# RWKV chunk transitions formed in bulk: W, P, Q and R ahead of the chunk loop, and small products laid on four 64x64 quarters of the PE array

## The chip, the core and the metric

The kernel runs on one core of a Trainium2 chip. A core has a matrix engine (TensorE, here PE, with its weight loads listed apart as PEld), three engines for element-wise work (VectorE or DVE, ScalarE or ACT, GpSimd or POOL) and DMA queues, which it issues from SyncE (SP). Matrix products are written to PSUM, an accumulator memory of eight banks; DVE and ACT carry them from there to SBUF. The metric is the time of one execution on the device in microseconds (us).

## The reference

Two layers, 512 tokens of 1024 channels, float32. Each layer normalises, projects, runs four mixers on the projection and mixes their outputs. The change lies in one of the four, an RWKV-7 time mix of 8 heads of 64 channels, run in both directions:

```
def _wkv7_scan(r, w, k, v, a, bb):
    def step(S, inp):
        r_t, w_t, k_t, v_t, a_t, b_t = inp
        sa = jnp.einsum("bhvk,bhk->bhv", S, a_t)
        S = S * w_t[:, :, None, :] + sa[..., None] * b_t[:, :, None, :] + v_t[..., None] * k_t[:, :, None, :]
        return S, jnp.einsum("bhvk,bhk->bhv", S, r_t)
    _, y = lax.scan(step, S0, (tm(r), tm(w), tm(k), tm(v), tm(a), tm(bb)))
```

The state S is a 64x64 matrix for each head. The other mixers are a Mamba-2 scan, differential attention and grouped-query attention.

## The kernel before

A layer runs in three parts: the RWKV mixer (`rwkv`), with the attention mixers woven into it; the Mamba mixer (`ssd`); the output projection (`accumulate`, `finish`). `rwkv` walks over four **blocks** j, each two heads (index e, 64 channels on each half of the 128 partitions), both directions d and all 512 tokens as 8 **chunks** of 64. So a block has 2 x 2 x 8 = 32 chunk problems.

In chunk form the scan of a block becomes these products, all 64x64x64 in float32 (the trace shows each such product as two matmul records and two weight loads):

- `products`: A and B matrices within a chunk (tile `pa`, 128 columns each), masked by DVE into `AT[0]` (from b) and `AT[1]` (from k).
- `turned`: v and the b, k matrices with tokens on the partitions (tiles `p5`, in the trace `p<-cst,lv`, and `pt`), carried by ACT into V2 and BKT.
- The inverse T of a unit triangular matrix: its 16x16 diagonal blocks are solved on DVE (15 pairs of small operations, lines 541 and 543), between transposes of 32x32 blocks on DVE (lines 528, 549, 551). Then come one product M (tile `ch<-DN,AT`) and three products that refine T (`ch<-DT,Mp`, `ch<-TT,Mp`), each followed by a DVE addition (line 571).
- Bulk terms: x (`px`), KV (`pk`), Y0 (`py`).
- The **chain** over the 8 chunks cc. With S the state of one chunk it forms X = a S + x (tile `bk`, DVE line 624), U = T X (`bk`, DVE copy line 635), S' = lambda (b U + S) + KV (`bk`, DVE lines 633 and 640), and adds r S and (b r) U to the output bank (`yb`). These are three steps that wait for each other, each a small group of products and a DVE operation.

Two things fill the time between these steps. `ahead()` advances the element-wise preparation of the next block (`prep`) and the normalisation of the last one (`norm`) by one piece. `fill(us)` advances attention work (tiles `pjt`, `pjc`, `sc`, `ptp`, `ob`) by a credit of about that many us; `fill.scale` is set so that 98% of 299.5 us of such work is spent in the four blocks. The constants F_SV (15 solve steps), F_MG (5 bulk steps) and F_CH (24 chain steps) say how the credit is shared out. The program text is then put in order by a scheduler that lets an instruction pass another that is not ready by its own reckoning; on the chip each engine works its list strictly in that order.

PSUM banks: two for projections (`pj`), two that all small work shares (`g`), one for attention (`ga`), two for the chain (`ch0`, `ch1`), one for the output (`yb`).

In `products` the matmul goes from half e of the partitions to half e or to the other half, e ^ m, so that four consecutive products use four different 64x64 quarters of the array. In the other products one block uses two quarters, on a diagonal.

Of the kernel before, what the change touches and what calls it, by code (L numbers as in the profile page):

```python
# [19 lines left out]
L = 512  # L20
# [7 lines left out]
F_SV = 1.5  # L28
F_MG = 2.4
F_CH = 1.7  # L30
# [7 lines left out]
C_LAG = 4  # L38
N_PR = 3
# [3 lines left out]
END = 0.98  # L43
# [13 lines left out]
C_N = C_TH + 2  # L57
# [18 lines left out]
def trunk(ctx: ExitStack, tc: tile.TileContext, x_in, win, wwd, wdt, wout, w2a, cols, rows, sscal, consts, out, dbg=None,  # L76
# [32 lines left out]
    nomask = cst[:, C_NOM:C_NOM + 64]  # L109
    th = [cst[:, C_TH + n:C_TH + n + 1] for n in range(2)]  # L110
# [141 lines left out]
    def rwkv(i, lay, pw, ps, rp, fill):  # L252
# [36 lines left out]
        AR = rp.tile([128, 4, 2, 8, 64], F32, tag="AR", name="AR")  # L289
# [26 lines left out]
        def prep(j):  # L316
# [6 lines left out]
            s["a"], s["r"] = Aa, Ar = AR[:, j % 2], AR[:, 2 + j % 2]  # L323
# [11 lines left out]
            for d in range(2):  # L335
# [41 lines left out]
                BKf = rp.tile([128, 17 * 64], F32, tag="BK", name="BK", bufs=2)  # L377
                G.memset(BKf[:, 0:64], 0.0)
                s["BK"].append(BKf)
                BK = BKf[:, 64:].rearrange("p (c a t) -> p c a t", c=8, a=2)  # L380
# [4 lines left out]
                G.tensor_tensor(BK[:, :, 1, :], v3(kp), il, op=ALU.mult)  # L385
# [4 lines left out]
                V.scalar_tensor_tensor(BK[:, :, 0, :], v3(b1), -0.5, il, op0=ALU.mult, op1=ALU.mult)  # L390
# [23 lines left out]
        AT = [rp.tile([128, 2, 8, 2, 64], F32, tag=f"AT{n}", name=f"AT{n}") for n in range(2)]  # L414
        BKT = rp.tile([128, 2, 2, 8, 64], F32, tag="BKT", name="BKT")
        V2 = rp.tile([128, 2, 8, 64], F32, tag="V2", name="V2")

        ba = AT[0][:, :, :, 0, :]
        half = [slice(0, 64), slice(64, 128)]

        def products(j, c0, n):

            ar = AR[:, j % 2:j % 2 + 3:2]
            for d in range(2):
                BK = sts[j]["BK"][d][:, 64:].rearrange("p (c a t) -> p c a t", c=8, a=2)
                pa = [ps.tile([128, n, 128], F32, tag="g", name="pa") for _ in range(2)]
                for cc in range(n):
                    for m in range(2):
                        for e in range(2):
                            mm(pa[m][half[e ^ m], cc, :].rearrange("p (a t) -> p a t", a=2), BK[half[e], c0 + cc, m, :],  # L430
                               ar[half[e], :, d, c0 + cc, :], True, True)
                for m in range(2):
                    V.tensor_tensor(AT[m][:, d, c0:c0 + n].rearrange("p c a t -> p c (a t)"), pa[m],
                                    rmask.unsqueeze(1).to_broadcast([128, n, 128]), op=ALU.mult)

        def turned(j):
            BK, v = sts[j]["BK"], sts[j]["v"]
            for d in range(2):

                p5 = ps.tile([128, 8, 64], F32, tag="g", name="p5")  # L440
                for cc in range(8):
                    for e in range(2):
                        mm(p5[half[1 - e], cc, :], v[d][half[e], cc * 64:cc * 64 + 64], ident[half[e], half[e]], True, True)
                S.activation(V2[:, d], p5, AF.Copy)
                yield
            for d in range(2):
                for e in range(2):
                    pt = ps.tile([128, 8, 64], F32, tag="g", name="pt")

                    n = 7 + e  # L450
                    for cc in range(n):
                        PE.transpose(pt[:, cc, :], BK[d][half[e], (2 * cc + 1 - e) * 64:(2 * cc + 3 - e) * 64],
                                     ident[half[e], half[e]])
                    S.activation(BKT[:, d, e, 0:n], pt[:, 0:n], AF.Copy)
                    yield
# [47 lines left out]
        fill.scale = END * 299.5 / (4 * (15 * F_SV + 5 * F_MG + 24 * F_CH) + F_GN)  # L503
        products(0, 0, 4)
        products(0, 4, 4)
        ys = None
        for j in range(4):
            Aa, Ar, lamC = (sts[j][n] for n in ("a", "r", "lamC"))
            ahead.gens = [turned(j)]
# [5 lines left out]


            sv = rp.tile([128, 1024], F32, tag="sv", name="sv", bufs=1)
# [3 lines left out]
            DT = rp.tile([128, 2, 8, 64], F32, tag="dt", name="DT", bufs=1)  # L521
            DN = rp.tile([128, 2, 8, 64], F32, tag="dn", name="DN", bufs=1)
            G.memset(sv[:, 768:1024], 0.0)
            G.memset(sv[:, 768:1024:17], 1.0)
            quad = [(slice(32 * q, 32 * q + 32), slice(32 * (q % 2), 32 * (q % 2) + 32)) for q in range(4)]
            unit = lambda t, q: t[quad[q][0], :, :, quad[q][1]].rearrange("p d c (h t) -> p t h (d c)", h=2)
# [4 lines left out]
            bam = AT[0].rearrange("p d c a t -> p (d c) a t")[:, :, 0, :]  # L531
            G.tensor_tensor(bam, bam, nomask.unsqueeze(1).to_broadcast([128, 16, 64]), op=ALU.mult)
            G.memset(DT, 0.0)
            G.memset(DN, 0.0)
            for jj in range(15):
                ahead()
                fill(F_SV)
# [8 lines left out]
            for h in range(2):  # L546
                V.tensor_scalar(Dx[:, :, h, :], Ti, th[h], None, op0=ALU.mult)
            for q in range(4):
                V.transpose(out=unit(DN, q), in_=Dx[quad[q][0]].rearrange("p t h s -> p s h t"))
            for q in range(4):  # L550
                V.transpose(out=unit(DT, q), in_=Dx[quad[q][0]])
            ahead()
            fill(F_MG)
            chd = lambda d: ps.tile([128, 8, 64], F32, tag=f"ch{d}", name=f"ch{d}")
            both = [(cc, e) for cc in range(8) for e in range(2)]

            Mp = rp.tile([128, 2, 8, 64], F32, tag="sv", name="Mp", bufs=1)
            for d in range(2):
                pm = chd(d)
                for cc, e in both:  # L560
                    mm(pm[half[e], cc, :], ba[half[e], d, cc, :], DN[half[e], d, cc, :], True, True)
                S.activation(Mp[:, d], pm, AF.Copy)
            TT = rp.tile([128, 2, 8, 64], F32, tag="dn", name="TT", bufs=1)
            for n in range(3):
                ahead()
                fill(F_MG)
                for d in range(2):
                    ph = chd(d)
                    for cc, e in both:
                        mm(ph[half[e], cc, :], Mp[half[e], d, cc, :], (TT if n else DT)[half[e], d, cc, :], True, True)  # L570
                    V.tensor_tensor(TT[:, d], ph, DT[:, d], op=ALU.add)
            ahead()
            fill(F_MG)

            KV = rp.tile([128, 2, 8, 64], F32, tag="sv", name="KV", bufs=1)
            Y0 = rp.tile([128, L], F32, tag="dt", name="Y0", bufs=1)
            for d in range(2):
                px = ps.tile([128, 8, 64], F32, tag="g", name="px")
# [853 lines left out]
```

## Time and profile before

| | |
|---|---|
| time, median of 3 runs | 1848.87 us (1847.95 to 1852.3) |
| the profiled execution: time, span of its instructions | 1854.4 us, 1852.6 us |
| PE busy | 1642.2 us, 89% of the span |
| DVE, ACT, POOL busy | 1163.1 us (63%), 810.5 us (44%), 698.9 us (38%) |
| the four blocks of layer 0 lie at | 113 to 675 us |
| those of layer 1 at | 1031 to 1593 us |

Busy is the union of an engine's instruction times. Of matmuls the trace gives start and a modelled end, so many records overlap: the time that a group of them holds the engine is read from the start of its first record to the start of the next group. "Idle before" is time in which the engine had nothing running, put down to what released the next instruction. The profile gives the clock that TensorE was granted, as a share of 2.4 GHz; its levels here are 1.0 and 0.5 (1.2 GHz).

### The profile page before, as it was taken

How to read it: one execution, taken by the hardware profiler on the slowest of the kernel's cores; microseconds unless marked ns; L12 is line 12 of the kernel's file. 1: busy time of each engine (PE TensorE's matmuls, PEld its weight loads, DVE VectorE, ACT ScalarE, POOL GpSimd, SP SyncE). 2: the span in 40 equal slices, each digit the busy share in tenths (PEclk: the TensorE clock that was granted, in tenths of full speed). 3: DMA queues.
4: the chain of work that ended last, by engine and by line, in shares of the span. 5: the costliest groups of instructions: out<-in, count | busy, mean ns of one | idle time of the engine just before them, and what ended most of it. 6: DMA issues, size and time to landing. Idle time of an engine off the chain costs nothing. (4 is left out here: it accounts for less than half of the span.)

```text
span 1852.6 us, 35939 instructions
## 1 busy us (share of the span) xinstructions
PE 1642.2 (89%) x14616; PEld 1325.0 (72%) x14616; DVE 1163.1 (63%) x2426; ACT 810.5 (44%) x1566; POOL 698.9 (38%) x728
## 2 busy tenths in 40 slices
PE   7887989998988999988897799899889898999888
PEld 6576767776767877766785677687677677778666
DVE  4587586676665437886256865956856744378852
ACT  4644245435524255442346442563444242554431
POOL 4443233334242334543354332433432323345333
PEclk9898999999989999989999989999999899999899
DMA  4111101111001114122431111011110011231223
GB/s 152 60 40 39 35 24 42 49 41 44 26 24 47 42 54 135 64 73 88 134 104 52 32 39 36 29 37 50 37 44 30 24 47 36 81 112 53 86 86 114
DMA packets 57510, 108.41 MB, mean 59 GB/s; under 512 B 6784, under 2 KB 8832, under 8 KB 57344
## 3 DMA queue, kind: packets, MB, share of 16 engines
q1 hardware_dynamic: 57344, 106.11, 17.7%
q8 instruction: 114, 1.87, 0.4%
q14 instruction: 52, 0.43, 0.1%
HBM read 95.60 MB, written 10.49 MB: 57 GB/s over the span
## 5 line engine op out<-in xcount | busy, mean ns | idle before, releaser
L144 POOL TENSOR_TENSOR wlo<-wf,whi 128x512 fp32r<-128x512 f32 x228 | 315.6, 1389 | 444.7 <-ACT whi L143 360.2
L82 PE MATMUL pjt<-whi,hhi 128*128 128x256 f32 x960 | 297.5, 310 | 13.0 <-ACT raw L269 6.5
L82 PE MATMUL pjt<-wlo,hhi 128*128 128x256 f32 x960 | 293.7, 307 | 1.1 <-POOL wlo L144 1.1
L82 PE MATMUL pjt<-whi,hlo 128*128 128x256 f32 x960 | 287.9, 300 | 0.0
L143 ACT ACTIVATE whi<-wf 128x512 fp32r<-128x512 f32 x228 | 141.3, 628 | 215.8 <-PE pjt L82 104.0
L82 PEld LDWEIGHTS pjt<-whi,hhi 128*128 128x128 f32 x960 | 192.6, 201 | 34.6 <-issue 9.0
L82 PEld LDWEIGHTS pjt<-wlo,hhi 128*128 128x128 f32 x960 | 192.6, 201 | 11.4 <-issue 6.5
L82 PEld LDWEIGHTS pjt<-whi,hlo 128*128 128x128 f32 x960 | 193.0, 201 | 8.8 <-issue 5.6
L82 PE MATMUL pjc<-hhi,whi 128*128 128x512 f32 x384 | 161.8, 421 | 9.0 <-ACT raw L269 5.2
L82 PE MATMUL pjc<-hhi,wlo 128*128 128x512 f32 x384 | 159.7, 418 | 0.0
L82 PE MATMUL pjc<-hlo,whi 128*128 128x512 f32 x384 | 158.1, 412 | 0.0
L872 DVE TENSOR_REDUCE nm<-sc 128x1 f32<-128x512 f32 x96 | 65.9, 687 | 84.6 <-PE sc L82 78.1
L875 ACT ACTIVATE p<-sc,nm 128x512 f32<-128x512 f32 x96 | 65.9, 686 | 115.1 <-DVE nm L872 114.7
L82 PE MATMUL mix<-whi,ylo 128*128 128x512 f32 x256 | 106.1, 414 | 5.4 <-DVE ylo L1216 5.4
L82 PE MATMUL sc<-qT,qT 64*128 64x512 f32 (+1 forms) x256 | 101.7, 494 | 7.2 <-ACT y L1055 3.8
L82 PE MATMUL mix<-whi,yhi 128*128 128x512 f32 x256 | 101.0, 417 | 5.1 <-ACT yhi L1215 5.1
L82 PE MATMUL mix<-wlo,yhi 128*128 128x512 f32 x256 | 104.4, 408 | 0.0
L82 PEld LDWEIGHTS pjc<-hhi,whi 128*128 128x128 f32 x384 | 76.5, 199 | 32.9 <-issue 6.6
L82 PEld LDWEIGHTS pjc<-hhi,wlo 128*128 128x128 f32 x384 | 76.3, 199 | 21.4 <-issue 4.2
L82 PEld LDWEIGHTS pjc<-hlo,whi 128*128 128x128 f32 x384 | 76.5, 199 | 15.7 <-issue 0.3
L1224 POOL TENSOR_TENSOR wlo<-wf,whi 128x512 fp32r<-128x512 f32 x32 | 44.4, 1390 | 112.3 <-ACT whi L1223 107.6
L1223 ACT ACTIVATE whi<-wf 128x512 fp32r<-128x512 f32 x64 | 40.4, 631 | 94.0 <-PE mix L82 59.3
(331 smaller groups left out, 3828.6 us busy)
## 6 DMA issues: line engine op xcount, KB each, us to landing
wf<-in_win_dram SPq DMA_DIRECT2D x224, 256.0 KB, 2.9
wf<-in_wout_dram SPq DMA_DIRECT2D x64, 256.0 KB, 2.6
y<-y_dram SPq DMA_DIRECT2D x24, 256.0 KB, 2.7
xt<-in_x_dram SPq DMA_DIRECT2D x8, 512.0 KB, 4.0
y_dram<-y SPq DMA_DIRECT2D x16, 256.0 KB, 2.7
y_dram<-rs SPq DMA_DIRECT2D x8, 256.0 KB, 2.1
x_dram<-t SPq DMA_DIRECT2D x8, 256.0 KB, 2.4
xt<-x_dram SPq DMA_DIRECT2D x4, 512.0 KB, 4.3
```

What stands on the lines that cost most here:

```text
L82: PE.matmul(o, lhsT, rhs, start=start, stop=stop, skip_group_check=skip)
L143: S.activation(hi, wf, AF.Copy)
L144: G.tensor_tensor(lo, wf, hi.bitcast(F32), op=ALU.subtract)
L872: V.tensor_reduce(nm, sc, axis=AX, op=ALU.max, negate=True)
L875: S.activation(p, sc, AF.Exp, bias=nm, accum_out=sm)
L1223: S.activation(hi, wf, AF.Copy)
L1224: (V if kt % 2 else G).tensor_tensor(lo, wf, hi.bitcast(F32), op=ALU.subtract)
```

## The change

Before the chunk loop, for all 32 chunk problems of a block, the change forms U0 = T X0, W = T a, the transition P = I + b W, the input Q = lambda (k v + b U0), the reader R = r + (b r) W and the output share Y0. A chunk of the chain is then S' = lambda P S + Q and y += R S: one product group in `bk`, one DVE operation, one group in `yb`. The chain's three steps of `fill` per chunk become one.

The bulk products run in the order (chunk pair cp, head e, chunk parity p), with e and p choosing the partition halves of operand and result, so that four consecutive ones use four quarters. The three refining products (`ph`) stay on two. a, b, k and v are turned by 128x128 transposes. Of the 12 DVE block transposes on 32 partitions three on 128 partitions remain; 16 ACT copies on 32 partitions rearrange the data around them. The F constants and C_LAG change with the number of steps. `products` for AT[1] moves to the head of its own block, for AT[0] to the end of the block before.

The core of the diff:

```diff
-F_SV = 1.5
-F_MG = 2.4
-F_CH = 1.7
+F_SV = 2.0
+F_MG = 2.5
+F_CH = 3.5
-C_LAG = 4
+C_LAG = 5
...
+        def products(j, m, tags=G2):
...
+                for cp, e, p in each:
+                    mm(pa[e][half[p], cp, :].rearrange("p (a t) -> p a t", a=2), BK[half[e], m, 2 * cp + p, :],
+                       ar[half[e], :, d, 2 * cp + p, :], True, True)
...
+        def turned(src, nm):
+
+            pt = ps.tile([128, 4, 128], F32, tag="g", name=nm)
+            for cp in range(4):
+                PE.transpose(pt[:, cp, :], src[:, cp * 128:cp * 128 + 128], ident)
...
             for q in range(4):
-                V.transpose(out=As[quad[q][0]].rearrange("p t (h s) -> p t h s", h=2), in_=unit(ba, q))
+                S.activation(thu(close, q), unit(ba, q), AF.Copy)
+            V.transpose(out=sv[:, 0:512], in_=close)
...
+            V.transpose(out=close.rearrange("p (t h s) -> p t h s", t=16, h=2), in_=Dx.rearrange("p t h s -> p s h t"))
             for q in range(4):
-                V.transpose(out=unit(DN, q), in_=Dx[quad[q][0]].rearrange("p t h s -> p s h t"))
+                S.activation(unit(DN, q), thu(close, q), AF.Copy)
...
+            for d, cp, e, p in every:
+                mm(pw[e][half[p], 4 * d + cp, :], TT[half[p ^ e], e, d, cp, :], A[half[p ^ e], e, d, cp, :], True, True)
...
+            for n, (d, cp, e, p) in enumerate(every):
+                mm(pq[p][half[e], 4 * d + cp, :], KT[half[p], e, d, cp, :], VT[half[p], e, d, cp, :], n < 4, False, True)
+            for d, cp, e, p in every:
+                mm(pq[p][half[e], 4 * d + cp, :], ba[half[p], e, d, cp, :], U0[half[p], e, d, cp, :], False, True, True)
...
+            for d in range(2):
+                pp = banks(C2 if d else G2, [128, 4, 128], "pp")
+                for cp, e, p in each:
+                    mm(pp[p][half[e], cp, :].rearrange("p (a t) -> p a t", a=2), W[half[p], e, d, cp, :],
+                       AT[0][half[p], e, d, cp, :, :], True, True)
+                for p in range(2):
+                    V.tensor_tensor(P[:, d, p::2, :], pp[p][:, :, 0:64], id64.unsqueeze(1).to_broadcast([128, 4, 64]),
+                                    op=ALU.add)
+                    V.tensor_tensor(R[:, d, p::2, :], pp[p][:, :, 64:128], Ar[:, d, p::2, :], op=ALU.add)
...
-                        for e in range(2):
-                            mm(bk[half[e], 0, :], Aa[half[e], d, cc, :], St[d][half[e], :], True, True)
-                ahead()
-                fill(F_CH)
...
-                        V.tensor_tensor(Xs, bk[:, 0, :], ba[:, d, cc, :], op=ALU.add)
-                    for e in range(2):
-                        mm(bk[half[e], 1, :], TT[half[e], d, cc, :], Xs[half[e]], True, True)
-                ahead()
-                fill(F_CH)
...
-                    V.tensor_copy(Us, bk[:, 1, :])
-                    if cc < 7:
-                        for e in range(2):
-                            mm(bk[half[e], 2, :], BKT[half[e], d, e, cc, :], Us[half[e]], True, True)
...
+                    if cc < 7:
+                        bk = ps.tile([128, 8, 64], F32, tag=f"ch{d}", name=f"bk{d}")
                         for e in range(2):
+                            mm(bk[half[e], 0, :], P[half[e], d, cc, :], St[d][half[e]], True, True)
+                        Sn[d] = rp.tile([128, 64], F32, tag=f"S{d}", name=f"S{d}", bufs=2)
+                        V.scalar_tensor_tensor(Sn[d], bk[:, 0, :], lamC[:, d, cc:cc + 1], Q[:, d, cc, :],
                                                op0=ALU.mult, op1=ALU.add)
                     for e in range(2):
-                        if cc:
-                            mm(yb[half[e], rev(d, cc)], St[d][half[e], :], Ar[half[e], d, cc, ::1 - 2 * d], False, True, True)
-                        mm(yb[half[e], rev(d, cc)], Us[half[e]], AT[0][half[e], d, cc, 1, ::1 - 2 * d], False, True, True)
+                        mm(yb[half[e], rev(d, cc)], St[d][half[e]], R[half[e], d, cc, ::1 - 2 * d], False, True, True)
+                St = Sn
+                step(2, F_CH)
```

How often a product stands in the whole program, before and after (as the program lists it, one for two records): in the chain `bk` 704 and `yb` 480, after it 192 and 224; 64x64 products of the bulk on two quarters 1248 (`p<-cst,lv`, `ch<-DN,AT`, `px`, `pk`, `py`), after it 2048 on four (`pm`, `px`, `pu`, `pw`, `pq`, `py`); products of 128 columns on four quarters 512 (`pa`), after it 768 (`pa`, `pp`); transposes of RWKV operands 240 of 64 rows, after it 256 of 128 rows; `ph` or `ch` refining products 768 both times.

The first place is the chain on PE. Before, in the second block of layer 0, one chunk stands as three groups with attention work between them (S is the state, `pjt` attention); the first and the last group:

```order
L82 MATMUL bk_3463<-S_3441,AR 64x64 x2
...
L82 MATMUL bk_3463<-Xs_3506,TT 64x64 x2
L82 MATMUL bk_3466<-Xs_3510,TT 64x64 x2
...
L82 MATMUL bk_3463<-Us_3557,BKT 64x64 x2
L82 MATMUL yb<-AR,S_3441 64x64
L82 MATMUL yb<-AT_434,Us_3557 64x64
```

After, a chunk of the same block is one group:

```order
L82 MATMUL pjt<-wlo,hhi 128x256
L82 MATMUL bk_3866<-S_3810,P 64x64 x2
L82 MATMUL yb<-R,S_3810 64x64 x2
L82 MATMUL bk_3873<-S_3817,P 64x64 x2
L82 MATMUL yb<-R,S_3817 64x64 x2
L82 MATMUL pjt<-whi,hhi 128x256
```

The first two groups and their waits are gone, and the third has lost its U products. The second place is PE at the end of the bulk part in the same block. Before:

```order
L82 MATMUL px<-V_437,AT_435 64x64 x32
L82 MATMUL pk<-V_437,BKT 64x64 x28
L82 MATMUL py<-hhi,cr 128x512
L82 MATMUL py<-AT_435,V_437 64x64 x32
L82 MATMUL yb<-hhi,cr 128x512
```

After (W, U and P, R come from DVE and ACT, out of PSUM, between these rows):

```order
L82 MATMUL pp<-AT_434,W 64x128 x15
L82 MATMUL py<-AT_435,VT 64x64 x16
L82 MATMUL py<-AT_434,U_3383 64x64 x16
L82 MATMUL yb<-R,Q 64x64 x4
L82 MATMUL p_3759<-low_290,w_2847 128x512
L82 MATMUL bk_3738<-Q,P 64x64 x2
```

No attention work stands between `pp`, the products `py` that need its two banks again, and the first two products that read R and P. The third place is DVE there, after:

```order
L639 TENSOR_TENSOR P<-pp,cst 128x4x64
L641 TENSOR_TENSOR R<-pp,AR 128x4x64
L651 TENSOR_TENSOR Y_3663<-py,Y_3663 128x256 x2
L671 SCALAR_TENSOR_TENSOR S_3741<-bk_3738,lamC,Q 128x64
L671 SCALAR_TENSOR_TENSOR S_3748<-bk_3745,lamC,Q 128x64
```

P and R stand there four times each in a row, then Y0, then the first two states.

## Rows read from the trace of the kernel before

**Rows 1.** Page, busy time of each engine.

```profile
PE 1642.2 (89%) x14616; PEld 1325.0 (72%) x14616; DVE 1163.1 (63%) x2426; ACT 810.5 (44%) x1566; POOL 698.9 (38%) x728
```

**Rows 2.** Stretches: block 1 of layer 0, and a PE wait in block 0.

```profile
core 0: us, PE busy (x) PEld busy (x) DVE busy (x) ACT busy (x) POOL busy (x), PEclk, DMA share, GB/s
240.00:387.00 147.00, 136.38 (x1478) 106.51 (x1478) 101.08 (x223) 70.85 (x128) 54.21 (x54) 0.98 0.13 40
139.60:150.60 11.00, 0.10 (x4) 0.00 (x0) 10.71 (x12) 3.55 (x7) 5.84 (x5) 0.66 0.16 52
```

**Rows 3.** Groups by line on PE: three that wait; after the second bar, idle before.

```profile
L82 PE MATMUL bk<-S,AR 64*64 64x64 f32 x448 | 34.8, 238 | 7.2 <-DVE S L640 7.2
L82 PE MATMUL bk<-Xs,TT 64*64 64x64 f32 x448 | 32.1, 241 | 16.8 <-DVE Xs L624 16.8
L82 PE MATMUL p<-bh,cr 128*128 128x512 f32 x32 | 16.6, 518 | 31.7 <-ACT bh L283 31.6
```

**Rows 4.** PE in order of time, three chain groups: start, us, instruction, count.

```profile
324.75 0.33 PE L82 MATMUL bk<-Us,BKT 64*64 64x64 f32 x4
...
325.36 0.50 PE L82 MATMUL p<-bh,cr 128*128 128x512 f32 x1
...
334.30 0.33 PE L82 MATMUL bk<-Us,BKT 64*64 64x64 f32 x4
...
335.19 0.50 PE L82 MATMUL sc<-qT,qT 64*128 64x512 f32 x1
...
342.63 0.28 PE L82 MATMUL pjt<-whi,hlo 128*128 128x256 f32 x1
342.75 0.28 PE L82 MATMUL pjt<-wlo,hhi 128*128 128x256 f32 x1
342.96 0.45 PE L82 MATMUL bk<-S,AR 64*64 64x64 f32 x8
343.34 0.39 PE L82 MATMUL pjt<-whi,hhi 128*128 128x256 f32 x1
343.56 0.28 PE L82 MATMUL pjt<-whi,hlo 128*128 128x256 f32 x1
```

**Rows 5.** Groups by line on PE: the bulk work that goes.

```profile
L452 PE MATMUL pt<-cst,BK 64*128 64x64 f32 x240 | 20.2, 233 | 0.4 <-ACT BKT L454 0.4
L82 PE MATMUL ch<-DN,AT 64*64 64x64 f32 x512 | 19.3, 223 | 3.4 <-DVE DN L549 3.4
L82 PE MATMUL p<-cst,lv 64*64 64x64 f32 x512 | 18.4, 221 | 1.3 <-DVE AT L433 1.3
L82 PE MATMUL px<-V,AT 64*64 64x64 f32 x512 | 17.3, 220 | 0.0
L82 PE MATMUL py<-AT,V 64*64 64x64 f32 x512 | 16.6, 220 | 0.0
L82 PE MATMUL pk<-V,BKT 64*64 64x64 f32 x448 | 15.3, 220 | 0.0
```

**Rows 6.** PE in order of time: 128-row transposes, single records, products on four quarters.

```profile
478.52 0.63 PE L897 MATMUL ptp<-cst,p 128*128 128x128 f32 x4
479.08 0.33 PE L82 MATMUL bk<-S,AR 64*64 64x64 f32 x4
...
485.79 0.22 PE L82 MATMUL yb<-AT,Us 64*64 64x64 f32 x1
485.80 0.22 PE L82 MATMUL yb<-AR,S 64*64 64x64 f32 x1
...
499.78 1.10 PE L82 MATMUL pa<-AR,BK 64*64 64x128 f32 x32
500.82 0.39 PE L82 MATMUL pjt<-wlo,hhi 128*128 128x256 f32 x1
```

**Rows 7.** Groups by line on DVE and ACT: nearest operations to those added.

```profile
L549 DVE STREAM_TRANSPOSE DN<-sv 32x512 f32<-32x512 f32 x32 | 38.7, 1209 | 1.3 <-DVE sv L547 0.5
L444 ACT ACTIVATE V<-p 128x512 f32<-128x512 f32 x16 | 9.5, 596 | 28.5 <-PE p L82 28.5
L844 DVE TENSOR_TENSOR of<-po,exT 128x256 f32<-128x256 f32 x24 | 9.0, 416 | 1.6 <-PE po L82 1.6
```

More of the change, by code (lines that the diff above doesn't have):

```diff
@@ L56 @@
 C_TH = C_NOM + 64
-C_N = C_TH + 2
+C_I64 = C_TH + 2
+C_N = C_I64 + 64
 C_MNEG = C_N
@@ L410, in prep @@
                 yield
[L414 to L418, printed above, removed]
+        AT = [rp.tile([128, 2, 2, 4, 2, 64], F32, tag=f"AT{n}", name=f"AT{n}") for n in range(2)]
+        VT = rp.tile([128, 2, 2, 4, 64], F32, tag="VT", name="VT")
         half = [slice(0, 64), slice(64, 128)]
[L421 to L434 removed]
@@ new lines, in rwkv, with banks @@
+        each = [(cp, e, p) for cp in range(4) for e in range(2) for p in range(2)]
+        every = [(d, cp, e, p) for d in range(2) for cp, e, p in each]
+        ba, br = AT[0][:, :, :, :, 0, :], AT[0][:, :, :, :, 1, :]
+        ka, kr = AT[1][:, :, :, :, 0, :], AT[1][:, :, :, :, 1, :]
+        def banks(tags, shape, nm):
+            return [ps.tile(shape, F32, tag=t, name=nm) for t in tags]
+        G2, C2 = ("g", "g"), ("ch0", "ch1")
+        zeros = cr[:, 272:273].to_broadcast([128, 128])
@@ L502, in rwkv @@
         fill.credit = 0.0
-        fill.scale = END * 299.5 / (4 * (15 * F_SV + 5 * F_MG + 24 * F_CH) + F_GN)
-        products(0, 0, 4)
-        products(0, 4, 4)
+        fill.scale = END * 299.5 / (4 * (15 * F_SV + 9 * F_MG + 7 * F_CH) + F_GN)
+        for _ in products(0, 0):
+            pass
         ys = None
         for j in range(4):
-            Aa, Ar, lamC = (sts[j][n] for n in ("a", "r", "lamC"))
-            ahead.gens = [turned(j)]
+            s = sts[j]
+            Ar, lamC = s["r"], s["lamC"]
+            ahead.gens = [by_tokens(j)]
             if j:
@@ L514, in rwkv, with step @@
                 ahead.gens.append(prep(j + 1))
+            def step(n, us):
+                ahead(n)
+                fill(us)
+            unit = lambda t, q: t[quad[q][0], :, :, :, quad[q][1]].rearrange("p e d c (h t) -> p t h (e d c)", h=2)
+            thu = lambda t, q: t[quad[q][0]].rearrange("p (t h u) -> p t h u", t=16, h=2)
             sv = rp.tile([128, 1024], F32, tag="sv", name="sv", bufs=1)
@@ new lines, in rwkv @@
+                for e in range(2):
+                    S.activation(unit(DT, (q + 2 * e) % 4)[:, :, :, 8 * e:8 * e + 8], thu(close, q)[:, :, :, 8 * e:8 * e + 8],
+                                 AF.Copy)
+            step(1, F_MG)
+            Mp = tokens("Mp", "sv")
+            pm = banks(G2, [128, 8, 64], "pm")
+            for d, cp, e, p in every:
+                mm(pm[e][half[p ^ e], 4 * d + cp, :], ba[half[p], e, d, cp, :], DN[half[p], e, d, cp, :], True, True)
+            S.activation(flat(Mp[:, 0]), pm[0], AF.Copy)
@@ new lines, in rwkv @@
+            step(1, F_MG)
+            Y0 = rp.tile([128, 2, 4, 64], F32, tag="kt", name="Y0", bufs=1)
+            for d in range(2):
+                py = banks(C2 if d else G2, [128, 4, 64], "py")
+                for n, (lhs, rhs, (cp, e, p)) in enumerate((l, r, x) for l, r in ((VT, kr), (U0, br)) for x in each):
+                    mm(py[p ^ d][half[e], 3 - cp if d else cp, :], lhs[half[p], e, d, cp, :],
+                       rhs[half[p], e, d, cp, ::1 - 2 * d], n < 4, False, True)
+                for b in range(2):
+                    if d:
+                        V.tensor_tensor(Y0[:, b], py[b], Y0[:, b], op=ALU.add)
+                    else:
+                        S.activation(Y0[:, b], py[b], AF.Copy)
@@ L650, in rwkv @@
+                St = Sn
+                step(2, F_CH)
             ahead.finish()
-            while j < 3 and made < 8:
-                n = min(4, 8 - made)
-                products(j + 1, made, n)
-                made += n
             ys = rp.tile([128, L], F32, tag="tmp", name="ys", bufs=3)
-            V.tensor_tensor(ys, yb, Y0, op=ALU.add)
+            for b in range(2):
+                sl = lambda t: t.rearrange("p (c b t) -> p c b t", c=4, b=2)[:, :, b, :]
+                V.tensor_tensor(sl(ys), sl(yb), Y0[:, b], op=ALU.add)
```

198 lines of the change are left out of this document (90 added, 108 removed).

## Prediction

> **What bounds the kernel now.** I read the page's busy times first [rows 1]: PE is busy for 89% of the span, no other engine for more than 63%. A busy share alone says little for an engine whose records overlap, so I went on to stretches. In a whole block of the part that changes (block 1 of layer 0), PE is busy for 136.4 of 147 us at a granted clock of 0.98, DVE for 101 and ACT for 71 [rows 2]. So the blocks are bound by the work in PE's list and, for the rest, by waits in it. The groups by line tell who waits [rows 3]: the chain's second step for X (16.8 us in all), its first for S (7.2), and the small product `p<-bh` of the next block's preparation (31.7). The longest of these last is the second stretch of [rows 2]: 11 us in which PE does 0.10 us of work and DVE 10.7. `bh` stands there behind DVE's preparation, and that behind block transposes of about 1.2 us each [rows 7]. The granted clock falls to half (1.2 GHz) after PE has stood still like that; the mean of this stretch is 0.66.
>
> From this: an edit inside a block is worth the time by which it shortens PE's list, plus or minus waits. How the credit of `fill` is shared out moves attention work but removes none of it.
>
> **The chain.** What a small group costs PE is read in order of time at full clock [rows 4]. Attention matmuls follow each other by 0.12 us (342.63 to 342.75). From 342.75 to 343.56 there are two of them and one group of 8 records (four products): 0.81 - 2 x 0.12 = 0.57 us. Of this 0.38 runs from the group's own start to the next start; the other 0.19 is lost on both sides, at the change from large to small products. A group of 24 records runs from 334.30 to 335.19, 0.89, so with that loss 1.08. One of 16 records takes 325.36 - 324.75 = 0.61, so 0.80.
>
> A full chunk before is 8 + 8 + 24 records in three groups: 0.57 + 0.57 + 1.08 = 2.22 us. The first chunk has no state to read (0.57 + 0.80 = 1.37), the last makes none (0.57 + 0.57 + 0.80 = 1.94). A block: 6 x 2.22 + 1.37 + 1.94 = 16.6 us. After, six chunks have one group of 16 records and the last output one of 8: 6 x 0.80 + 0.57 = 5.4 us. That is 11.2 us less per block, **90 us** less in eight.
>
> **The bulk.** What goes is 107.1 us in all, 13.4 per block (the six groups of [rows 5]). What comes depends on what a product costs on four quarters. On two, `px` needs 17.3 us for 256 products of 64 columns, 67.6 ns each, or 1.06 ns per column. On four, `pa` runs 32 records, 16 products of 128 columns, from 499.78 to 500.82 [rows 6]: 65 ns each, or 0.51 ns per column. So the trace already shows four quarters at twice the rate of two. No row shows a product of 64 columns on four quarters; its cost lies between 32.5 ns (half of `pa`) and 67.6 ns (no better than `px`). I take 32.5, since `pa` is the one row with the same use of the array. Per block then: 256 products (`pm`, `px`, `pu`, `pw` 32 each, `pq`, `py` 64 each) 8.3 us; 32 products `pp` of 128 columns 2.1; 32 transposes of 128 rows, four in 479.08 - 478.52 = 0.56 us [rows 6], 4.5. Sum 14.9 against 13.4: 1.5 us more per block, **12 us** in all. The refining products and `pa` are the same in number and cost.
>
> A rule of the Trainium skill speaks against the 32.5 ns: "TensorE: Matmul & The Clock Gate", section "Wait — 56ns, not 53.3ns?", says that the distance from one matmul's start to the next never falls below about 25 ns, however few the columns. By that, an estimate, 512 records per block would take 12.8 us in place of 8.3, and the forecast would be 36 us later, about 1807. The trace does not bear it out where two quarters take turns: two records start at 485.79 and 485.80 [rows 6].
>
> **DVE and ACT.** DVE loses 12 transposes for 3 and 44 small operations of the chain in each block. A transpose on 128 partitions is not in the trace: 1.21 us if the partition groups go side by side [rows 7], 4.84 if one after the other; at either price DVE has no more to do than before, and it isn't what bounds a block. ACT gets 18 copies of 512 elements at 0.596 [rows 7] and 16 of 256, between half of that and all of it, and gives up 11 of 512: 8.9 to 13.7 us more per block. On 70.9 of 147 that still leaves it well under PE. So I cost both engines' work itself at nothing: PE's list of 136 us per block covers it. Not covered is what PE waits for.
>
> **Waits.** Gone: those for X (16.8). Of those for S (7.2) and `bh` (31.7) I take about two thirds, since DVE has fewer transposes in front and the chain asks for fewer small operations: 40 us in all; at most 55.7, at least 17. New: at the end of the bulk part PE has nothing but `pp`, `py` and the first state in a row (second place in the order), while DVE adds P and R in eight operations on 128x256 out of PSUM, 0.416 each by the nearest row [rows 7], 3.3 us. The second half of `pp` and the first of `py` cover 2 x 1.04 of it; the rest and the first state behind two Y0 additions make some 2 us per block. What is queued behind is the whole of PE's list, attention included. The other new hand-overs (the ACT copies ahead of `pm`, W, U0, X0) mostly have attention work in between; I allow 3 us per block for them, between nothing and all of ACT's added 13.7. New waits so far: 5 us per block, 40 in all, with 16 and 126 as bounds. Old and new cancel, and I enter **0**, with bounds of -40 and about +100.
>
> **Sum.** -90 + 12 + 0 = -78 us. Against the profiled execution's 1854.4 us (1.8 outside its span) that gives 1776; this execution was 5.5 above the median of the runs, 1848.87, so the forecast is 1771 us.
>
> **Rivals.**
>
> *DVE's relief counts in full* (chance 0.16). All 55.7 us of the listed waits go and only 16 come; the clock then falls less often, too. 1771 - 40 = 1731 us. For it speaks the 11 us stretch, which DVE alone filled; against it, that half of that DVE work is preparation which stays.
>
> *PSUM's emptying takes the place of the chain* (0.12). If all added ACT time (about 11 us) and the 2 us at P and R stand in PE's way, 13 us per block, 104, against 40 gone: 1771 + 64 = 1835. For it: the bulk steps follow each other directly, each through a copy out of PSUM. Against it: ACT is idle for half of a block. "TensorEngine Tiling (Array Packing)" of the Trainium skill, section "PSUM Bottleneck", warns of just this after a speed-up by tiling. Above 15.5 us of new waits per block it would even be slower than before; I give that 0.04 more.
>
> *Records cannot follow faster than in any long run shown* (0.08). The runs `px` and `pa` both average 32 to 34 ns per record, though columns and quarters differ by two each. If that is a floor for issue, small products gain nothing from four quarters: 256 x (67.6 - 32.5) = 9.0 us per block, 72: 1843 us, at the edge of no change. Against it: the single records 10 ns apart [rows 6].
>
> *Four quarters need one common stream* (0.05), the case on the other side. In `pa` before, the two products that share a half of the rows also stream the same columns of AR. After the change each has its own, in all bulk products and in `pa` itself. If that halves the rate, the 64-column products cost 9.0 us more per block, `pp` 2.1 and `pa` (64 products) 4.2: 15.3, 122 in all: 1893 us, slower. It decides from about 60 ns per 64-column product, with `pa` slowed in step. Nothing in the rows speaks for it, and nothing excludes it.
>
> **How the numbers follow.** The forecast itself has 0.55, with 1750 to 1795 as its own range. No change is what lies within 0.3%, 5.5 us, about what a measurement of this kernel can tell. Faster: 0.55 + 0.16 + 0.12 and a third of the 0.08 makes 0.86; the same 0.05; slower 0.05 + 0.04 = 0.09. The range for 8 in 10 runs from a little below the best case to the edge of no change, 1726 to 1843.
>
> **What would show it.** Right: the chain takes one group of some 0.8 us per chunk and no wait for X or U; a run of 64 records of `pw` or `pu` takes about 1 us rather than 1.9; PE's busy time falls by some 70 us. Wrong: `pu` runs at 30 ns per record; `pa` slows; PE stands at `py` or at the first `bk` behind P and R for more than 3 us per block, or at `pm` behind the 32-partition copies; `p<-bh` still waits 11 us in block 0.

## The result, and the profile after

The changed kernel takes 1868.01 us (median; 1859.53 to 1874.69), the kernel before beside it 1852.3: a ratio of 1.0081, 95% interval 1.0052 to 1.0110. It is slower, where 1771 had been forecast. The profiled execution is the fastest of its runs, 1859.5 us. Its page, span and busy time of each engine, to be read beside [rows 1]:

```profile
span 1857.7 us, 36925 instructions
PE 1600.4 (86%) x15200; PEld 1305.4 (70%) x15200; DVE 1031.5 (56%) x2098; ACT 937.2 (50%) x1750; POOL 694.7 (37%) x712
```

PE does 41.8 us less and stands still 46.9 us more (span less busy time, 257.3 against 210.4). Busy time itself hides a third change, since the granted clock fell from 0.939 to 0.927. To part the three I took for every PE record of the trace the time to the next record's start, less the idle part, and put it down to the clock granted at the time; what passed at half clock (1.2 GHz) counts half as work and half as loss. The time before the first record and behind the last, some 17 us together, is left out.

| us | before | after | difference |
|---|---|---|---|
| PE's list, at full clock | 1546.9 | 1488.2 | -58.7 |
| loss at half clock | 94.7 | 111.7 | +17.0 |
| PE idle | 193.6 | 240.8 | +47.2 |

Together that is 5.5 us, the difference of the two profiled executions. The medians lie 16 us apart; the other 10 are in no trace.

All of the added idle time lies in the blocks (115.5 before, 163.6 after). Worked out from the gaps between PE's records, by the product that came after each gap:

| idle in the blocks, us | before | after |
|---|---|---|
| preparation and norm (`p<-bh` and its like) | 35.2 | 17.6 |
| chain (`bk`, `yb`) | 24.4 | 16.6 |
| products and turns (`pa`, `pv<-cst`) | 3.9 | 22.2 |
| solve and bulk (`pm`, `ph`, `px` to `py`) | 4.5 | 28.0 |
| attention (`ptp`, `pqt`, `sc`, `pjt`, `pjc`) | 47.5 | 79.2 |

The groups by line on PE name the waits (behind the second bar the idle time before, and its releasers). Those of [rows 3] have gone or shrunk; these stand in their place:

```profile
L82 PE MATMUL sc<-qT,qT 64*128 64x512 f32 (+1 forms) x256 | 103.2, 502 | 20.5 <-DVE qT L938 7.2 <-ACT p L900 5.2 <-ACT y L1059 3.7
L82 PE MATMUL pa<-AR,BK 64*64 64x128 f32 x1024 | 63.7, 321 | 16.6 <-DVE AT L444 16.6
L922 PE MATMUL ptp<-cst,p 128*128 128x128 f32 x256 | 42.6, 287 | 35.5 <-DVE p L1057 16.1 <-ACT p L900 15.1 <-ACT bh L284 2.5
L82 PE MATMUL ph<-DN,Mp 64*64 64x64 f32 x1024 | 37.9, 227 | 12.9 <-DVE DN L597 12.9
L82 PE MATMUL bk<-S,P 64*64 64x64 f32 x320 | 25.9, 243 | 12.3 <-DVE S L671 12.3
L82 PE MATMUL pu<-X,DN 64*64 64x64 f32 x512 | 17.7, 261 | 8.5 <-DVE X L606 6.6 <-ACT X L605 1.9
L82 PE MATMUL p<-bh,cr 128*128 128x512 f32 x32 | 15.8, 493 | 7.2 <-ACT bh L284 7.2
```

Next the changed kernel in order of time (start, duration, instruction, count): PE at one run of 64 records and at one chunk of the chain, then PE, DVE and POOL around the wait at 525 us.

```profile
329.63 1.11 PE L82 MATMUL pw<-A,DN 64*64 64x64 f32 x64
330.67 0.97 PE L82 MATMUL sc<-qT,qT 64*128 64x512 f32 x3
...
356.76 0.28 PE L82 MATMUL pjt<-wlo,hhi 128*128 128x256 f32 x1
356.97 0.33 PE L82 MATMUL bk<-S,P 64*64 64x64 f32 x4
...
357.37 0.28 PE L82 MATMUL yb<-R,S 64*64 64x64 f32 x4
357.58 0.39 PE L82 MATMUL pjt<-whi,hhi 128*128 128x256 f32 x1
...
523.02 2.28 POOL L127 TENSOR_TENSOR grr<-grv,cst 128x12 f32<-128x12 f32 x1
524.04 0.28 PE L82 MATMUL bk<-S,P 64*64 64x64 f32 x4
...
525.25 0.38 PE L82 MATMUL pjt<-whi,hhi 128*128 128x256 f32 x1
525.34 5.50 DVE L1022 SCALAR_TENSOR_TENSOR gqk<-gqk,grr,arow 128x128 f32<-128x128 f32 x12 [3.57 <-POOL grr L127]
527.29 0.82 POOL L951 TENSOR_TENSOR rt<-gqk,rot 128x96 f32<-128x96 f32 x2 [0.75 <-DVE gqk L1022]
530.77 0.41 DVE L954 TENSOR_TENSOR gqk<-gqk,rot 128x96 f32<-128x96 f32 x2
531.44 0.27 DVE L671 SCALAR_TENSOR_TENSOR S<-bk,lamC,Q 128x64 f32<-128x64 f32 x1
531.77 0.48 PE L82 MATMUL bk<-S,P 64*64 64x64 f32 x4 [6.14 <-DVE S L671]
```

Sixty-four records on four quarters take 330.67 - 329.63 = 1.04 us, 16 ns each, and a chunk of the chain 357.58 - 356.76 - 0.12 = 0.70. Then the wait: the state's DVE operation takes 0.27 us, and the last of its products started at 524.04. It stands in DVE's list behind attention work: twelve operations `gqk`, which had waited for POOL (`grr`) until 525.34, and four of the rotation, until 531.44. DVE's wait for POOL had put this work back by 3.57 us, but it was over when PE's began (531.77 - 6.14 = 525.63); PE stands 6.14 us while DVE works on the attention. The Trainium skill, "PSUM — Partial Sum Buffer", section "Engine vs sequencer instructions", calls the queues of these engines strict FIFO; the rows agree, for the ready operation did not pass the waiting one.

The kernel before has the same stand. Its wait for X in the same block lies behind the same twelve operations; first PE, then DVE:

```profile
529.08 0.48 PE L82 MATMUL bk<-Xs,TT 64*64 64x64 f32 x4 [4.50 <-DVE Xs L624]
```

```profile
522.69 5.52 DVE L997 SCALAR_TENSOR_TENSOR gqk<-gqk,grr,arow 128x128 f32<-128x128 f32 x12 [2.06 <-POOL grr L126]
```

So the wait for X did not go with X: here it is the new wait for S.

Two such stretches as windows (us, PE, PEld, DVE, ACT, POOL busy, then the granted clock, DMA share, GB/s):

```profile
525.00:532.00 7.00, 0.86 (x17) 0.49 (x11) 6.46 (x18) 0.00 (x0) 4.14 (x7) 0.84 0.23 75
387.00:397.00 10.00, 1.76 (x21) 1.32 (x23) 9.42 (x25) 2.12 (x4) 3.54 (x3) 0.64 0.23 79
```

In the second, 8.24 us of waiting at `pa`: DVE works through the solve steps, which stand ahead of the masks that would free `pa`'s banks. Four of these steps, from 385.69 to 392.38 us, took 1.18 to 1.25 us where the others take about 0.2, each of them begun while POOL was in an operation (see the last section). The clock falls in both.

### The profile page after: what moved, and what is told of

Same layout as the page of the kernel before. It is cut to its first block, busy times and chain, and to the rows that moved or that the text cites. A ratio compares the mean times of both kernels' runs of the same rounds, so it can differ in the third digit from the quotient of the medians.

```text
span 1857.7 us, 36925 instructions
## 1 busy us (share of the span) xinstructions
PE 1600.4 (86%) x15200; PEld 1305.4 (70%) x15200; DVE 1031.5 (56%) x2098; ACT 937.2 (50%) x1750; POOL 694.7 (37%) x712
## 5 line engine op out<-in xcount | busy, mean ns | idle before, releaser
L82 PE MATMUL pjt<-whi,hhi 128*128 128x256 f32 x960 | 297.0, 309 | 10.6 <-ACT raw L270 9.5
L82 PEld LDWEIGHTS pjt<-whi,hhi 128*128 128x128 f32 x960 | 194.8, 203 | 26.7 <-ACT raw L270 10.6
L82 PEld LDWEIGHTS pjc<-hlo,whi 128*128 128x128 f32 x384 | 75.4, 196 | 16.7 <-issue 2.2
```

Source lines behind the costliest of these rows:

```text
L82: PE.matmul(o, lhsT, rhs, start=start, stop=stop, skip_group_check=skip)
```

## The experiments

**Is PE's list still the bound?** Two runs take work off it for which only a block's last addition waits, one puts work on. e13 drops the products into `yb` from the changed kernel, e14 from the kernel before:

```diff
-                    for e in range(2):
-                        mm(yb[half[e], rev(d, cc)], St[d][half[e]], R[half[e], d, cc, ::1 - 2 * d], False, True, True)
```

> The changed kernel without the products R S into yb (the output lacks the share of the states, all else is computed). Nothing but the block's last addition waits for them, so this takes 384 matmul records, about 20 us at full clock with the half clock's share, off PE's list and no wait away. Theory C (PE's list is still the bound, a us of it is worth a us): 17 to 25 us faster than the changed kernel, 1843 to 1851. Theory D (after the change PE's list is no longer what sets the pace, its gaps only grow): 0 to 8 us faster.

> The kernel before without its products into yb (both kinds; the output lacks them). They hold PE for 44 us in the blocks. Theories C and D both say that the kernel before is bound by PE's list: 35 to 50 us faster, 1802 to 1817. If it gains under 20 us, already the kernel before was not bound by it, and the premise of the forecast was false.

Measured: e13 1836.36 us, ratio to before 0.9928 (0.9904 to 0.9951), 32 us under the changed kernel (28 by the ratios), more than its list fell (1488.2 to 1468.0). The traces do not show the surplus: the profiled executions, the changed kernel's fastest and the slowest of e13, lie 13 us apart. e14 1818.10, 0.9823 (0.9792 to 0.9854), 34 us under before for 33 us of list (1546.9 to 1514.0); not the 44 us of occupation that I had expected. Theory D falls: in both kernels a us of list is still worth about a us, and the new waits came on top.

e1 undoes the order of the bulk products:

```diff
-        each = [(cp, e, p) for cp in range(4) for e in range(2) for p in range(2)]
+        each = [(cp, e, p) for e in range(2) for cp in range(4) for p in range(2)]
```

> The changed kernel with its bulk products in the order head, chunk pair, parity, so that consecutive products use two quarters of the array as before, not four. Theory A (the matrix list did get shorter, and the time was lost in waits for hand-overs and at half clock): the changed kernel's trace shows four records of 64 columns per 58 ns and four of 128 columns per 109 ns on four quarters; on two quarters only two records fit. Added work: 256 products x 29 ns x 8 blocks = 59 us, and 768 products of 128 columns x 54 ns = 42 us, 101 us of matrix work at full clock; where PE waits for DVE anyway, part of it is hidden: 50 to 100 us slower than the changed kernel. Theory B (four quarters buy nothing, the list is not shorter): within 15 us of the changed kernel.

Measured: 1883.50, 1.0171 (1.0132 to 1.0209), 15 us slower than the changed kernel, so far under the expectation. The run does not do what I meant: the scheduler wove the halves of the loop into each other, so that many quadruples stayed, and the list grew by 20.4 us, not 101; the loss at half clock grew by about as much, and PE's idle time fell by 14. Its verdict is only that these 20 us were not hidden.

**DVE's order.** e3 marks DVE's hand-overs (the refining additions, the copies of M, X0, U0 and W, the new states), e4 the masks of `pa` as well; every DVE instruction written after a marked one must stand behind it in the list. e7 does this to the kernel before, with its own hand-overs. One of e3's marks:

```diff
-                    V.tensor_tensor(flat(DN[:, e]), ph[e], flat(DT[:, e]), op=ALU.add)
+                    V.tensor_tensor(flat(DN[:, e]), ph[e], flat(DT[:, e]), op=ALU.add, first=True)
```

> The changed kernel, with DVE's hand-over operations (copies of M, X0, U0 and W, the refining additions, the new states) kept ahead of all DVE work that is written after them; no operation changes. Theory A: the waits of PE for the refining addition (12.9 us) and for X0 (6.6) go, and a part of the half clock after them: 15 to 30 us faster than the changed kernel. Theory B: within 5 us.

> As the run before, and the masks of the products A and B (AT out of pa) also kept ahead of the DVE work written after them, the solve steps above all. Theory A: the 16.6 us at pa go too, with their half clock: 30 to 50 us faster than the changed kernel, so 1818 to 1838 and faster than before. Theory B: within 5 us of the changed kernel. If the solve steps themselves are the path, what is won at pa is lost behind them: no faster than the run before.

> The kernel before with the same rule: X, U, the new states, the refining additions and the first inverse's transposes are kept ahead of DVE work written after them. If late hand-overs are a fault that the change brought in, the kernel before gains little: within 6 us, and at most the 17 us of its waits for X and 7 for S. If this order fault is in both kernels alike, it gains 15 us or more, and the change is no better beside it.

Measured: e3 1847.84, 0.9979 (0.9955 to 1.0003); e4 1847.17, 0.9968 (0.9947 to 0.9989); e7 1884.66, 1.0168 (1.0141 to 1.0196). The groups by line of e4 (lines of the kernel's body are 19 higher there, and DVE's all go by one line, L89):

```profile
L101 PE MATMUL pa<-AR,BK 64*64 64x128 f32 x1024 | 67.1, 328 | 5.1 <-DVE bb L89 3.8 <-DVE AT L89 1.3
L101 PE MATMUL ph<-DN,Mp 64*64 64x64 f32 x1024 | 35.3, 220 | 0.0
L101 PE MATMUL bk<-S,P 64*64 64x64 f32 x320 | 25.9, 236 | 5.9 <-DVE S L89 5.9
L101 PE MATMUL pu<-X,DN 64*64 64x64 f32 x512 | 12.9, 234 | 2.2 <-ACT X L624 1.8 <-DVE X L89 0.3
```

The named waits are gone (that for S is halved), and 1% of the time. But others grew. In e3 those at the solve and bulk products and in the chain fell from 44.6 to 15.6 us, and yet PE's idle time as a whole by only 5, since those at the attention, the preparation and the products rose; the half clock gave another 11. The masks gave next to nothing beside the hand-overs: idle time at products fell from 26.4 to 11.0 us from e3 to e4, and that at the attention rose from 87.9 to 97.7. In the kernel before, the same rule, on hand-overs of its own, costs 33 us (list +14, half clock +10, idle +7 in its trace). Late hand-overs are thus a fault of the changed kernel's order; as a rule for any kernel it is no good.

**DVE's stops for POOL.** DVE's waits for `rt` in the changed kernel (total, times, longest), and in the kernel before:

```profile
DVE qk L954 <- POOL rt L951: 46.0, 8, 11.1
```

```profile
DVE qk L929 <- POOL rt L926: 21.2, 4, 10.5
```

e9 moves these products to DVE, e10 does so in the kernel before, e11 adds the rule of e3:

```diff
-            G.tensor_tensor(view(t[:, 0:m, :]), view(x[:, :, 1 - h, :]), sin, op=ALU.mult)
+            V.tensor_tensor(view(t[:, 0:m, :]), view(x[:, :, 1 - h, :]), sin, op=ALU.mult)
```

> The changed kernel, with the two products by the sine in the attention's rotation (rt) on DVE instead of POOL. In the changed kernel's trace DVE stands 46 us waiting for rt (before the change 21), and PE's waits at 418, 525, 627 and 638 us lie behind such stops. Theory A (PE's new waits come from attention pieces that hold DVE's list): 10 to 25 us faster than the changed kernel, although DVE gets some 20 to 30 us more work. Rival: DVE's own work counts, slower by 5 us or more.

> The same edit in the kernel before, whose DVE stands only 21 us for rt, 10.5 of these ahead of the first block. Theory A: no gain or a small one, within 6 us. If it gains as much as the changed kernel does, the stops were a matter of both kernels and no cause of the difference.

> The changed kernel with the rotation on DVE and DVE's hand-overs ahead of what is written after them. Theory A: both cures reach different waits (at the refining additions the one, at the states and U0 the other), so 30 to 40 us faster than the changed kernel, about 1830, 20 us faster than before. If they cure the same waits: no better than the hand-over run, 1848.

Measured: e9 1839.06, 0.9900 (0.9877 to 0.9922), 29 us under the changed kernel. e10 1842.06, 0.9921 (0.9904 to 0.9938): the kernel before gains too, 13 us, more than expected. So about half of e9's gain belongs to both kernels and half to the change; with that edit in both, they are level (0.9900 and 0.9921, the intervals overlap). e11 1841.70, 0.9925 (0.9905 to 0.9944), no better than e9: the cures did not add.

What e9 cured is less than its expectation names. DVE's stops for `rt` are gone, but of the four waits of PE listed there, those at 418 and 627 us stand in e9 as in the changed kernel (4.57 and 3.17 us). That at 525 has changed its name: the wait at `bk<-S,P` is 0.0, and PE stands at the attention's transposes behind the same twelve operations and the rotation:

```profile
529.73 1.12 PE L933 MATMUL pqt<-cst,gqk 128*128 128x128 f32 x4 [6.98 <-DVE gqk L955]
```

Only the wait at 638 is gone. Over the whole trace the waits at `bk<-S,P` and `pqt<-cst,gqk` together go from 23.3 to 14.7 us; in the kernel before, those at `bk<-Xs,TT` and `pqt<-cst,gqk` go from 18.6 to 16.7 in e10. The attention's line in the changed kernel, e9, the kernel before and e10:

```profile
L933 PE MATMUL pqt<-cst,gqk 128*128 128x128 f32 x48 | 10.7, 363 | 11.0 <-DVE gqk L955 10.1 <-ACT qT L941 0.9
L933 PE MATMUL pqt<-cst,gqk 128*128 128x128 f32 x48 | 10.6, 360 | 14.7 <-DVE gqk L955 14.7
L908 PE MATMUL pqt<-cst,gqk 128*128 128x128 f32 x48 | 8.5, 304 | 1.8 <-DVE gqk L930 1.5
L908 PE MATMUL pqt<-cst,gqk 128*128 128x128 f32 x48 | 11.9, 395 | 16.7 <-DVE gqk L930 16.7
```

In all, e9's trace has 14 us less idle time on PE and 7 less loss at half clock. That DVE's stops for `rt` were the cause of the new waits is thus not shown; at 418, 525 and 627 us the trace speaks against it.

**Where the attention work falls.** e2 gives the changed kernel the old shares, e8 the kernel before shares like the new, e5 cuts the chain's step in two, e6 is e5 with the rule of e3, e12 e2 with it:

```diff
-F_SV = 2.0
-F_MG = 2.5
-F_CH = 3.5
+F_SV = 1.5
+F_MG = 2.4
+F_CH = 5.1
```

> The changed kernel with the attention work shared out as before: 1.5 per solve step, 2.4 per bulk step, and three chain steps of 1.7 in one, 5.1 per chunk. No operation is added or removed. If the new waits come from where single pieces of attention work happen to fall in DVE's list, the time moves by more than 10 us either way; if they come from the bulk part itself whatever lies around it, it stays within 10 us of the changed kernel's 1868.

> The kernel before with attention work shared out like that of the changed kernel: 39 in 100 beside the solve steps (before 30), 29 beside the bulk steps (before 16), 32 beside the chain (before 54). No operation altered. It shows what a mere change of place of the attention work is worth. If the placing is worth as much as the whole change (the changed kernel took 12 us less with the old shares), the time moves by 10 us or more; if not, within 6 us.

> The changed kernel with the chain's one step of attention work and preparation per chunk (3.5) cut in two: after each direction's products one piece of preparation and 1.75 of attention work. Nothing is added. Theory A1 (the coarse step is to blame: with one lump per chunk the attention chain of scores, softmax and transposes runs bare, and PE waits for it): the waits at ptp, pqt and sc, which grew from 19 to 35 us in layer 0, fall back by half, 15 to 30 us faster than the changed kernel. Rival A2 (the waits lie in the bulk and solve part, where nothing is altered here): within 6 us.

> Both edits together: two steps per chunk and DVE's hand-over operations ahead of what is written after them. If the two causes are separate, the gains add: the 20 us of the hand-over run and what the two steps alone give. If both only move the same waits about, it is no faster than the better of the two.

> The changed kernel with the old shares of attention work and the hand-overs first. If the two gains (12 and 20 us) add, 1836; if each is only another throw of where pieces fall, no better than 1848.

| run | us | ratio to before (95%) |
|---|---|---|
| e2 | 1855.68 | 1.0034 (1.0002 to 1.0066) |
| e8 | 1855.16 | 1.0015 (0.9996 to 1.0034) |
| e5 | 1864.22 | 1.0073 (1.0049 to 1.0096) |
| e6 | 1856.90 | 1.0023 (1.0001 to 1.0046) |
| e12 | 1850.22 | 0.9970 (0.9955 to 0.9985) |

e5 speaks against A1: a finer step in the chain is worth nothing measurable, and the idle time at the attention went from 79.2 to 85.4 us, not down. e8 shows that placing alone moves waits between classes: in the kernel before, the attention's rose from 47.5 to 86.1 us, those of preparation and chain fell from 59.6 to 25.0, and the time stayed. So the new shares alone give the kernel before as much waiting at the attention as the changed kernel has; but the old shares do not take it from the changed kernel, where e2 has 98 us of it. e2 gains 12 us (9 by the ratios, whose intervals overlap), at the border set for it, and not in the waits: its list is 10 us shorter and its loss at half clock 7 lower, while PE's idle time is 12 us longer. e6 and e12 gain no more than e3 alone.

**Copies, and all cures together.** e18 has ACT do DVE's four copies of the bulk part (`V.tensor_copy(flat(X0[:, 1]), px[1])` and its like become `S.activation(..., AF.Copy)`). e15 is the rotation on DVE with hand-overs and masks first, e16 the rotation with the old shares, e17 all three.

> The changed kernel with the four copies out of PSUM that DVE does in the bulk part (one half of M, X0, U0 and W, 0.68 us each) done by ACT behind its own half. DVE's stops then hold none of them. The forecast's rival (emptying PSUM takes the place of the chain, ACT short of time): slower by 5 us or more. Theory A (the waits are DVE's stops, 6.6 us at pu among them): 5 to 12 us faster than the changed kernel.

> The changed kernel with the rotation on DVE, and hand-overs and masks ahead of DVE work written after them. If the waits at pa (8.3 us in block 2 of each layer) and at pv are a loss of their own: 8 to 20 us faster than with the rotation alone, 1820 to 1831. If a cured wait only turns up elsewhere, as in the two runs of hand-overs so far: 1835 to 1845.

> The changed kernel with the rotation on DVE and the old shares of attention work. If both gains add: 29 + 12 us, 1827. If the shares only threw the pieces to other places: 1835 to 1850.

> The changed kernel with all three edits: rotation on DVE, old shares, hand-overs and masks first on DVE. The last gave 5.5 us beside the rotation and 5.5 beside the old shares. If it adds here too: 1822 to 1826; if the waits turn up elsewhere: 1828 to 1835.

| run | us | ratio to before (95%) |
|---|---|---|
| e18 | 1861.22 | 1.0054 (1.0033 to 1.0076) |
| e15 | 1833.57 | 0.9909 (0.9881 to 0.9936) |
| e16 | 1829.79 | 0.9892 (0.9862 to 0.9922) |
| e17 | 1809.90 | 0.9782 (0.9759 to 0.9805) |

e18 is not slower, so ACT is not short of time; that it is faster than the changed kernel lies within both intervals. In its trace the waits at the solve and bulk products fell from 28 to 11 us, and those at the attention rose by 14. By the ratios neither e15 nor e16 is clear of e9 (0.9900); only with all three edits does the time fall further, and below what either theory had for it. e17 is the fastest version found, 41 us under before and 58 under the changed kernel. Its page and groups by line on PE:

```profile
span 1806.1 us, 36905 instructions
PE 1587.9 (88%) x15200; PEld 1289.7 (71%) x15200; DVE 1016.6 (56%) x2154; ACT 936.3 (52%) x1750; POOL 675.7 (37%) x656
```

```profile
L101 PE MATMUL pa<-AR,BK 64*64 64x128 f32 x1024 | 62.0, 315 | 1.5 <-DVE AT L89 1.5
L101 PE MATMUL ph<-DN,Mp 64*64 64x64 f32 x1024 | 38.0, 226 | 0.0
L101 PE MATMUL bk<-S,P 64*64 64x64 f32 x320 | 26.8, 247 | 0.1
L101 PE MATMUL pu<-X,DN 64*64 64x64 f32 x512 | 11.9, 222 | 0.3 <-DVE X L89 0.3
```

Its list is that of the changed kernel (1487.8), its idle time 201.0 and its loss at half clock 99.7: with waits of nearly the size of before, the shorter list shows. The idle time of the classes products and turns, solve and bulk, and chain, 66.8 us in the changed kernel, is 13 us there. Two of its edits touch work outside the change; against the kernel before with the same rotation (e10) the ratio is 0.9782 / 0.9921 = 0.986. The kernel before was not run with the rotation and other shares together, nor was an order sought for it as for the changed one, so what of e17 is the change's own worth, and what a lucky fall of the pieces, is not shown beyond that.

## Why the prediction was wrong

**The step that failed is "Waits": old and new cancel, and 0 was entered.** They came to +47 us of idle time and +17 at half clock, 64 in all, inside the stated bounds (-40 to about +100) but far from the value taken. (Their upper bound should have been 126 - 17 = 109.) Of the old ones, that at `p<-bh` went almost whole in the blocks (25.5 to 0.3), though 10.2 came at `pv<-bh`. Those for X were counted as gone with X, but they lay behind the attention's `gqk` in DVE's list, and that stayed: behind it PE now waits for S, and at `pqt` (18.6 us at X and `pqt<-cst,gqk` before, 23.3 at S and `pqt<-cst,gqk` after). The classes of preparation and chain gave 25 us together, not 40. The new ones were sought in the wrong place. P, R and Y0 cost PE 3.3 (at `py`) and 4.4 us (at the first `bk`), 8 against the 16 estimated. What I had covered by "attention work in between" were DVE's hand-overs at `ph`, `pu` and the chain and the masks at `pa`, and there other work was the trouble that stood ahead of them in DVE's list: the attention's at the chain, the solve steps at `pa`. That these waits hang on DVE's order, e3, e4 and e17 show, in which they are gone or far smaller. I had costed DVE by its busy time and found it idle enough; it was, and its hand-overs were late all the same. The attention's own waits, +32 us, had no term at all; no run of the changed kernel brought them back to the 47.5 of before (80.9 in e17), and their cause stays open: e8 shows as many in the kernel before.

**The chain** was right: the list outside the bulk fell by about as much as forecast. `bk` and `yb` hold PE for 72 us less at full clock, and the attention and other work around them for 22 less, since large and small products alternate less often: 94 against 90.

ACT's added work was mis-read: of the 16 copies on 32 partitions 8 have 512 columns, 1.10 us each, and 8 have 256, 0.65 each, so ACT's busy time grew by 15.8 us per block (937.2 against 810.5 in all), over the 8.9 to 13.7 allowed. By e18 it did no harm.

**The bulk** was mis-sized: 136 us come and 103 go, +33 against +12. The rate was not the fault: a whole run of `pw` takes 16 ns per record, two records for a product, just the 32.5 ns per product that I took. But such runs are rarely whole; the scheduler cuts them and each piece pays for its two ends, so that `pm` averages 30 ns per record where the whole run of `pw` has 16, and `pp` 42 where `pa` in one piece has 33 [rows 6]. The 128-row transposes came in 8 us cheaper. `pa` kept its rate; its 10.6 us more were half clock, but for 2.

**The rivals.** Four quarters do not need a common stream: `pw` with its own streams takes 16 ns. Nor is there a floor of 32 ns per record. By the 25 ns of "TensorE: Matmul & The Clock Gate" of the Trainium skill, section "Wait — 56ns, not 53.3ns?", 64 records would take 1.6 us, an estimate; the trace disagrees, with 1.04 for records that go to different quarters. PSUM's emptying as ACT's burden is not borne out (e18). The side of the result was that of the rival "PSUM's emptying takes the place of the chain", which had been sought at ACT's copies and had the chance 0.12 and 0.04; the place was mostly DVE's list.

**The signs named beforehand.** The chain's group, `pw`'s run and the missing X wait came out as "right"; PE's busy time fell by 42 rather than 70; of the listed "wrong" signs at `pu` (22 ns per record in the mean, at full clock), `py`, `pm`, `pa` and `p<-bh` none appeared. The X wait read as "right" only by its name. The list of signs lacked the one that mattered, a hand-over late in DVE's list.

## What to carry to other kernels

When a change makes products on one engine shorter, look at each hand-over and ask what stands ahead of it in the list of the engine that makes it, and what that in turn waits for; a low busy share says nothing about this. A wait that is gone from one line may stand at another: look at the same stretch of time, not at the name (X, S and `pqt` here). Part a result into list, clock and idle time before judging the idea: here the idea was worth 59 us, the waits and the half clock around it cost 64, and three small edits of order and place, found by trying on this kernel, brought back 58. An order that cures one kernel can harm the other (e7), so a cure is tried on both.

## What was not expected of the hardware

DVE turns 128x512 elements in 0.71 us where both sides are contiguous, less than the 1.21 of 32x512 with both sides permuted in [rows 7]; with a permuted input 128x512 take 1.11. POOL needs 2.28 us to raise 128x12 elements to a power, and DVE's list stood behind it. ACT needs 1.10 us to copy 32x512 elements into a permuted view, more than the 0.60 of 128x512 out of PSUM in [rows 7].

```profile
L572 DVE STREAM_TRANSPOSE sv<-sv 128x512 f32<-128x512 f32 x8 | 5.7, 711 | 5.9 <-ACT DN L571 5.9
L571 ACT ACTIVATE DN<-sv 32x512 f32<-32x512 f32 x32 | 35.5, 1109 | 6.0 <-DVE sv L569 5.3
```

A DVE operation that begins while POOL is in one can last until POOL's has ended. In the changed kernel's wait at `pa`:

```profile
389.65 0.22 DVE L563 TENSOR_TENSOR sv<-sv,ot 128x55 f32<-128x55 f32 x1
389.90 1.25 DVE L561 TENSOR_TENSOR ot<-sv 128x60 f32<-128x60 f32 x1
389.81 1.27 POOL L285 TENSOR_TENSOR bl<-ys,bh 128x512 fp32r<-128x512 f32 x1 [1.76 <-ACT bh L284]
```

The second row ends at 391.15, just behind POOL's 391.08. Of DVE's operations 132 took over 0.6 us longer than the shortest of their kind, 134 us in all, and every one of them began while POOL was in an operation. In the kernel before there are 152, with 152 us, so this is no cause of the difference; but where PE waits for DVE, it makes the wait longer: four of the solve steps here, and two of the twelve `gqk` at 525 us (1.35 us, the others 0.34 to 0.47).
